# A layer of seven-product matrix multiplications: paired additions joined, marks and buffers set anew

## The chip, the cores and the metric

The kernel runs on one core of a Trainium2 chip. A core has a tensor engine (PE) for matrix products, VectorE (DVE), ScalarE (ACT) and GpSimd (POOL) for work on tiles of 128 partitions, and queues that start transfers (DMA), here mostly that of SyncE (SP). The engines work side by side, each through its own queue in order. The metric is the time of one execution on the device in microseconds (us), as the median of several runs. Shorter is better.

## The reference

The reference is one hybrid decoder layer in float32, on 256 tokens of width 2048, with 256 memory tokens:

```python
q, k, v, g_ret, xr, yr, g_a, g_b = jnp.split(rmsnorm(h) @ w_in, offsets, axis=-1)
ret_out = silu(g_ret) * head_groupnorm(chunkwise_retention(rotary(q), rotary(k), v))
rnn_out = gelu(yr) * rg_lru(causal_dwconv(xr))
merged = sigmoid(g_a) * (ret_out @ w_proj_ret) + sigmoid(g_b) * (rnn_out @ w_proj_rnn)
h = h + merged @ w_mix_out
h = h + memory_cross_attention(rmsnorm(h), rmsnorm(mem), xa_w_q, xa_w_k, xa_w_v, xa_w_o)
up = causal_dwconv(rmsnorm(h) @ w_up); gate, val = split(up)
h = h + (silu(gate) * val) @ w_down
return rmsnorm(h)
```

`w_in` has 14336 columns, `w_up` 11264, `w_down` 5632 rows, every other large weight is 2048 by 2048. Nearly all arithmetic lies in these products of 256 tokens by a weight.

## The kernel before

**Products in parts.** Each float32 operand is split into a high and a low part, and a product is three matmuls: high by high, low by high, high by low. For weights `weight_parts` does this: ACT casts a piece of `raw` to `hi` (L364), DVE subtracts it for `lo` (L365). The pool of hi and lo tiles has six of each (`PART_BUFS`), a tile holds two blocks of 128 by 512.

**Chunks and pairs.** The weights stand in one array in the order of use and come in chunks of 1 MB into three `raw` tiles, by loads on SP (L237). `weight_plan` lists the products in order. A plain one has 512 output columns. A pair has two times 512; its chunk is two blocks of 128 rows by two blocks of columns, called b11, b12, b21, b22, and it has eight chunks for 2048 rows. A chunk of a pair is worked off in `steps_pair` in one of two ways. Plain, it is 8 block products by 3 matmuls, 24 in all, of 512 columns each. Marked, it is a Strassen-like form with 7 products, 21 matmuls. A marked chunk needs on the weight's side, in `seven_parts`, four sums of blocks (L385, one DVE operation of 512 columns each) and seven parts in place of four. The token sums of its left operand are made by `sums_of` (L463 to L474), once for each left operand and kept for later products with the same one. `MARKS` lists, pair by pair in the order of the plan, which of the eight chunks are marked.

**Banks and the end of a pair.** A pair's results gather in PSUM: three tiles of two banks (pool `pm`) and two small banks (pool `px`, also used by small products). After the last marked chunk four DVE operations (L538) combine four banks into two SBUF tiles `o1`, `o2`; at the end of the pair four additions of 512 columns (L549) add the two small banks, then the two halves of the tile that holds p2 and p4.

**Order.** A step is one chunk. `chunks` loads and splits two chunks ahead (`AHEAD`) and, after each chunk, runs what `later(n, fn)` has set due n + 1 steps on. `LAG` holds these numbers for the steps around: loads of the residual rows (`rows`, `rows_step`) and of the memory rows (`squares`), the normed memory (`memory`), the head rows (`heads`), transposed rows of merged, query and key (`merge_turn`, `query_turn`, `key_turn`), the attention products (`attend`). A transposition (`by_dma`) is an ACT copy into planes, two transposing DMAs on SP and an ACT copy back. Matmuls stay in the order of the program; a planner orders the other engines' queues by priority and by when operands and buffers come free, and `high_priority` pulls the end of a pair ahead. Buffers of 4 KB a partition come from the pool `bp` ("big", 29 of them), those of 2 KB from `tp` ("tmp", 10), used by token sums, rotations, head outputs and probabilities.

**Stages.** Retention inputs and gates (until about 300 us), the recurrent branch's inputs (to 505), its projection and the gates (to 714), the retention projection and mixing (to 884), memory attention (to 1248), the feed-forward part with up and down products in turn (to 1884), and the last down product, whose four column blocks are plain.

Of the kernel before, what the change touches and what calls it, by code (L numbers as in the profile page):

```python
# [14 lines left out]
ALU = mybir.AluOpType  # L15
AX = mybir.AxisListType

P = 128
# [16 lines left out]
WARM = 7  # L35
FREE = 300
LAG = dict(
    sums=3, two_heads=2, recur=3, gelu=6, merged=2, memory=3, memory_step=3, rnn=0, rnn_step=2,
    heads=7, heads_step=1, squares=5, squares_step=1, rows=12, rows_step=1, residual=3, gate=2,
    value=4, merge_turn=2, query_turn=3, key_turn=4, turn=3, attend=1, acc_m=0, acc_h=0,  # L40
)
EPS = 1e-6
GN_EPS = 1e-5
FF_PARTS = [4, 4, 3]
EARLY = [2, 2, 4, 4, 4]
MARKS = [
    ((2, 5, 6), (3,), (3, 5, 6),),
    ((2, 5), (2, 5, 6), (2, 5, 6),),
    ((2, 4, 6), (2, 5), (2, 5), (5,),),
    ((3,), (3, 5),),  # L50
    ((), (2, 5), (2, 3), (2, 5), (2, 5), (),),
    ((5, 6), (),),
    ((2, 4), (2, 5), (5,), (2, 5), (2, 5), (2, 5), (2, 5),),
    ((2, 3, 5), (5,), (2, 5), (2, 5), (2, 5), (2, 5),),
    ((2, 5, 6), (3, 5),),
]

O_Q, O_K, O_V, O_G = 0, 1024, 2048, 4096
# [105 lines left out]
def chunk(inputs, name, row, n, c):  # L164

    if isinstance(c, tuple):
        a, b = (chunk(inputs, name, row, n, one) for one in c[:2])
        order = (b[:, 0], a[:, 0], b[:, 1], a[:, 1]) if c[2] else (a[:, 0], a[:, 1], b[:, 0], b[:, 1])
        return np.stack(order, axis=1)
    w = np.asarray(inputs[name])[0][row : row + n * P, c : c + BW].reshape(n, P, BW)  # L170
    return w.transpose(1, 0, 2)
# [9 lines left out]
def hybrid_layer(  # L181
# [18 lines left out]

    cp = ctx.enter_context(tc.tile_pool(name="cp", bufs=1))
    wp = ctx.enter_context(tc.tile_pool(name="wp", bufs=2))
    bp = ctx.enter_context(tc.tile_pool(name="bp", bufs=29))
    tp = ctx.enter_context(tc.tile_pool(name="tp", bufs=10))
    sp_ = ctx.enter_context(tc.tile_pool(name="sp", bufs=2))
    pm = ctx.enter_context(tc.tile_pool(name="pm", bufs=3, space=bass.MemoryType.PSUM))
    px = ctx.enter_context(tc.tile_pool(name="px", bufs=2, space=bass.MemoryType.PSUM))
# [13 lines left out]
    def acc():  # L221
        return pm.tile([P, 2, BW], F32, tag="acc", name=nm("acc"))
# [155 lines left out]

    def seven_parts(raw):

        b12, b11, b22, b21 = (raw[:, i, :] for i in range(4))
        p1, p3 = weight_parts(raw[:, 1:3])
        (p2,) = weight_parts(raw[:, 3:4])
        for o, a, b in ((b11, b12, b11), (b12, b12, b22), (b22, b11, b22), (b21, b22, b21)):
            dve.tensor_tensor(out=o, in0=a, in1=b, op=ALU.add)  # L385
        q3, q1 = weight_parts(raw[:, 0:2])
        q2, q4 = weight_parts(raw[:, 2:4])
        return [p1, p3, p2, q1, q3, q2, q4]

# [62 lines left out]
    def gemm_n(*args):  # L452
        return ended(steps_n(*args))
# [36 lines left out]
    def steps_pair(w, row, st, nk, c1, c2):  # L490

        seven = plan[gemms[0]][3][2]
        last = max(seven)
        banks, begun = {}, set()
        banks["p2"], banks["p4"] = (lambda a: (a[:, 0, :], a[:, 1, :]))(acc())
        banks["x3"], banks["n"] = (small((P, BW)) for _ in range(2))

        def rows_of(name, left, right, end):

            o = banks[name]  # L500
            for i, (a, b) in enumerate(((0, 0), (1, 0), (0, 1))):
                mm(o, left[a], right[b], start=name not in begun, stop=end and i == 2, skip_group_check=True)
                begun.add(name)

        o1 = o2 = None
        for k0, n, parts in chunks(nk, w, row, (c1, c2, seven)):
            k2 = k0 // KH
            for i in seven:
                if k2 < i <= k2 + LAG["sums"] and (not isinstance(st, list) or i < len(st)):
                    sums_of(st[i])  # L510
            if isinstance(st, Pairs):
                st[min(nk // KH - 1, k2 + 2)]
            t = st[k2]
            own = [
                [(t[:, j, i * P : (i + 1) * P], t[:, j, S + i * P : S + (i + 1) * P]) for j in range(2)]
                for i in range(2)
            ]
            if k2 in seven:
                if "p1" not in banks:
                    for a, b in (("p1", "p6"), ("p7", "x5")):  # L520
                        two = acc()
                        banks[a], banks[b] = two[:, 0, :], two[:, 1, :]
                ts = sums_of(t)
                s3, s1, s2, s4 = ((ts[:, 0, i, :], ts[:, 1, i, :]) for i in range(4))
                lefts = (own[0][0], s4, own[0][1], s1, s3, s2, own[1][1])
                for name, l, r in zip(("p1", "x3", "p2", "x5", "p7", "p6", "p4"), lefts, parts):
                    rows_of(name, l, r, k2 == last and name in ("p1", "x5", "p7", "p6"))
                if k2 == last:
                    o1, o2 = (big([P, 2, BW], s="o") for _ in range(2))
                    with tc.high_priority(FREE):  # L530
                        act.copy(o1[:, 0, :], banks["p1"])
                        for o, a, b, op in (
                            (o2[:, 0, :], o1[:, 0, :], banks["p6"], ALU.add),
                            (o1[:, 1, :], o2[:, 0, :], banks["p7"], ALU.add),
                            (o2[:, 1, :], banks["x5"], o1[:, 1, :], ALU.subtract),
                            (o2[:, 0, :], banks["x5"], o2[:, 0, :], ALU.subtract),
                        ):
                            dve.tensor_tensor(out=o, in0=a, in1=b, op=op)  # L538
            else:
                end = k0 + n == nk  # L540
                blocks = list(enumerate((("p2", "p4"), ("x3", "n"))))
                for b, names in reversed(blocks) if end else blocks:
                    for tt, name in enumerate(names):
                        for j in range(KH):
                            rows_of(name, own[tt][j], parts[b * KH + j], end and j == KH - 1)
            yield o1, o2
        with tc.high_priority(FREE):
            for o, a in ((o2[:, 0, :], "x3"), (o2[:, 1, :], "n"), (o1[:, 0, :], "p2"), (o1[:, 1, :], "p4")):
                dve.tensor_tensor(out=o, in0=o, in1=banks[a], op=ALU.add)  # L549

    def pair(*args):
        return ended(steps_pair(*args))
# [43 lines left out]
            for tt in range(2):  # L596
                act.mul(a[:, tt, :], a[:, tt, :], r[:, tt : tt + 1])

    def turned_rows(a, r, then, wait=1, urgent=True):

        rows = big([P, 2, BW], s="rows")
        with tc.high_priority(FREE) if urgent else nullcontext():
            for tt in range(2):
                dve.tensor_scalar_mul(rows[:, tt, :], a[:, tt, :], r[:, tt : tt + 1])  # L604
        by_dma(rows, then, wait)

    def split_pair(src, scale=None):
# [228 lines left out]
    for g in range(2):  # L836
        dec = big([P, 4, S], s="dec")
        vs, turned = [], ([], [])
        for b, o in enumerate((O_Q, O_K)):

            def rotate_both(f, o=turned[b]):
                o.append(rotated(f[:, 0:2, :]))
                later(0, lambda: o.append(rotated(f[:, 2:4, :])))

            a = gemm_n("w_in", 0, xs, NT, o + g * BW) if g + b else q0
            turned_rows(a, rs0, rotate_both, 2 - b if g + b else 3, g + b > 0)
            if b == 1:
                sp.dma_start(
                    out=dec,
                    in_=consts[:, C_DEC + g * 4 * S : C_DEC + (g + 1) * 4 * S].rearrange("p (h s) -> p h s", s=S),  # L850
                )
            if g == 0:
                v = gemm_n("w_in", 0, xs, NT, O_V + b * BW) if b else ended(v_steps)
                vs.append(split_rows(v, rs0))
        if g == 1:
            vs += [split_rows(v, rs0) for v in pair("w_in", 0, xs, NT, O_V + 1024, O_V + 1024 + BW)]
        qr, kr = turned
        gates = []
        c = O_G + g * 1024
        for a in pair("w_in", 0, xs, NT, c, c + BW):  # L860
            t = big([P, 2, BW], s="gate")
            for tt in range(2):
                act.activation(t[:, tt, :], a[:, tt, :], AF.Silu, scale=rs0[:, tt : tt + 1])
            gates.append(t)
        retain(g, qr, kr, vs, dec, gates)
# [73 lines left out]
    for b in range(4):  # L939
# [33 lines left out]
                dve.tensor_tensor(out=o, in0=xr[0][:, cs, :], in1=f[:, cs, :], op=ALU.mult)  # L973
                rnn.append(split_pair(o))

        turned_rows(gemm_n("w_in", 0, xs, NT, O_XR + b * BW), rs0, conv_x)
        turned_rows(gemm_n("w_in", 0, xs, NT, O_YR + b * BW), rs0, gelu_y, LAG["gelu"])


    def tanh_rows(t, a):  # L980
# [134 lines left out]
    def split_block(f, out, seven=()):  # L1115
        for pr in range(2):
            with_sums(out, seven, f[:, 2 * pr : 2 * pr + 2, :])
        return out
# [22 lines left out]
    def attend(b, v):  # L1141
# [4 lines left out]
        for tt in range(2):  # L1146
            cs = slice(tt * P, (tt + 1) * P)
            for kt in range(2):
                product(
                    a[:, tt, :], (phi[:, kt, cs], plo[:, kt, cs]), [t[:, kt, :] for t in v], kt == 0, kt == 1  # L1150
                )
        turned_rows(a, shares[b], lambda f: split_block(f, osp, marks_of("xa_w_o")))

    turned_pair("xa_w_k", ms, 0, rsms[0], keys)
    token_sums.clear()
# [215 lines left out]
```

## Time and profile before

| | us |
|---|---|
| median of 3 runs | 1964.05 (1963.98 to 1964.17) |
| the profiled execution | 1962.41 |
| its span | 1960.6 |
| PE busy | 1947.5 |
| weight loads busy (PEld) | 1616.5 |
| DVE busy | 1683.2 |
| ACT busy | 1426.2 |

The profile is of one execution. A group is named by line, engine, operation and the tiles it writes and reads, with shapes, count, busy time and mean duration, then the idle time of its engine just before and what ended that. An arrow in a view of waits points to the one waited for. A line is often that of a helper: all matmuls of the products are L266, all splits of weights L364 and L365. "sm" is a small bank, "acc" a tile of two banks, "ts" a token sum, "s" a split left operand. DMA moved 219 GB/s on average; the granted tensor clock was full throughout.

### The profile page before, as it was taken

How to read it: one execution, taken by the hardware profiler on the slowest of the kernel's cores; microseconds unless marked ns; L12 is line 12 of the kernel's file. 1: busy time of each engine (PE TensorE's matmuls, PEld its weight loads, DVE VectorE, ACT ScalarE, POOL GpSimd, SP SyncE). 2: the span in 40 equal slices, each digit the busy share in tenths (PEclk: the TensorE clock that was granted, in tenths of full speed). 3: DMA queues.
4: the chain of work that ended last, by engine and by line, in shares of the span. 5: the costliest groups of instructions: out<-in, count | busy, mean ns of one | idle time of the engine just before them, and what ended most of it. 6: DMA issues, size and time to landing. Idle time of an engine off the chain costs nothing.

```text
span 1960.6 us, 24200 instructions
## 1 busy us (share of the span) xinstructions
PE 1947.5 (99%) x8756; PEld 1616.5 (82%) x8756; DVE 1683.2 (86%) x2251; ACT 1426.2 (73%) x1746; POOL 35.2 (2%) x33
## 2 busy tenths in 40 slices
PE   9999999999999999999999999999999999999998
PEld 8888888888888888888888888888878888878886
DVE  6897987888799997997888668888999989998886
ACT  7666758999655766788688677887786588875783
POOL 0000011000000000000000000000000000000000
PEclk9999999999999999999999999999999999999999
DMA  9756667765555565867676656666667767677673
GB/s 337 240 215 173 205 243 205 207 226 191 199 206 195 223 240 195 308 221 243 205 220 222 211 188 202 200 231 220 204 215 229 250 217 223 207 219 253 215 238 128
DMA packets 198344, 429.82 MB, mean 219 GB/s; under 512 B 142160, under 2 KB 146768, under 8 KB 153168
## 3 DMA queue, kind: packets, MB, share of 16 engines
q1 hardware_dynamic: 197072, 424.09, 64.5%
q0 software_dynamic: 1152, 4.19, 1.2%
q8 instruction: 68, 1.11, 0.2%
q14 instruction: 52, 0.43, 0.1%
HBM read 388.39 MB, written 2.10 MB: 199 GB/s over the span
## 4 chain that ended last, share of the span: by engine, by line
PE 91%; DVE 4%; ACT 2%; issue 1%; DMA 1%; POOL 0%; POOLq 0%; DVEq 0%; SPq 0%; ACTq 0%
PE acc L266 63%; PE sm L266 28%; DVE lo L365 2%; DMA raw<-in_wall 1%; ACT hi L364 1%; DVE fv L1185 0%; DVE o L538 0%; ACT f L588 0%; DVE raw L385 0%; ACT pl L575 0%; DVE fo L1194 0%; ACT o L1311 0%; DVE o L549 0%; DMA raw<-in_head 0%; DVE fg L1185 0%
## 5 line engine op out<-in xcount | busy, mean ns | idle before, releaser
L365 DVE TENSOR_TENSOR lo<-raw,hi 128x1024 fp32r<-128x1024 f32 (+1 forms) x846 | 973.9, 1178 | 190.1 <-ACT hi L364 182.9
L364 ACT CAST hi<-raw 128x1024 fp32r<-128x1024 f32 (+1 forms) x846 | 829.4, 1012 | 368.3 <-DVE raw L385 109.6
L266 PE MATMUL acc<-hi,s 128*128 128x512 f32 (+1 forms) x3540 | 1085.1, 388 | 1.6 <-DVE s L612 1.1
L266 PEld LDWEIGHTS acc<-hi,s 128*128 128x128 f32 x3540 | 661.5, 188 | 138.1 <-DVE s L612 1.9
L266 PE MATMUL acc<-lo,s 128*128 128x512 f32 (+1 forms) x1770 | 686.2, 388 | 1.3 <-DVE lo L365 1.3
L266 PE MATMUL sm<-hi,s 128*128 128x512 f32 x1520 | 468.1, 389 | 1.1 <-DVE o L549 1.1
L266 PEld LDWEIGHTS acc<-lo,s 128*128 128x128 f32 x1770 | 332.3, 188 | 70.8 <-DVE lo L365 2.5
L266 PEld LDWEIGHTS sm<-hi,s 128*128 128x128 f32 x1520 | 285.2, 188 | 60.8 <-issue 1.5
L266 PE MATMUL sm<-lo,s 128*128 128x512 f32 x760 | 295.7, 389 | 0.0
L385 DVE TENSOR_TENSOR raw<-raw 128x512 f32<-128x512 f32 x264 | 181.4, 687 | 4.0
L588 ACT COPY f<-pt 128x1024 uint16<-128x1024 uint16 x128 | 166.4, 1353 | 9.5 <-DMA pt<-pl 9.5
L266 PEld LDWEIGHTS sm<-lo,s 128*128 128x128 f32 x760 | 142.7, 188 | 29.6
L266 PE MATMUL acc<-hi,ts 128*128 128x512 f32 x396 | 121.9, 389 | 0.0
L266 PEld LDWEIGHTS acc<-hi,ts 128*128 128x128 f32 x396 | 74.3, 188 | 15.4
L266 PE MATMUL acc<-lo,ts 128*128 128x512 f32 x198 | 77.4, 391 | 0.2 <-DVE lo L365 0.2
L575 ACT COPY pl<-o 128x1024 uint16<-128x1024 uint16 x64 | 62.6, 1040 | 2.9 <-DVE o L1043 2.2
L575 ACT COPY pl<-rows 128x1024 uint16<-128x1024 uint16 x44 | 43.8, 1042 | 17.6 <-DVE rows L604 17.5
L1311 ACT ACTIVATE o<-o,ro 128x512 f32<-128x512 f32 x44 | 30.1, 718 | 20.0 <-DVE o L549 19.5
L266 PEld LDWEIGHTS acc<-lo,ts 128*128 128x128 f32 x198 | 37.1, 188 | 9.0 <-DVE lo L365 1.5
L538 DVE TENSOR_TENSOR o<-o,acc 128x512 f32<-128x512 f32 x64 | 43.5, 680 | 0.5
L1185 DVE SCALAR_TENSOR_TENSOR fg<-f,pf,fg 128x255 f32<-128x255 f32 (+1 forms) x88 | 39.1, 478 | 4.5 <-ACT fg L1183 4.2
L549 DVE TENSOR_TENSOR o<-o,sm 128x512 f32<-128x512 f32 x64 | 42.3, 678 | 0.2
(184 smaller groups left out, 1106.5 us busy)
## 6 DMA issues: line engine op xcount, KB each, us to landing
raw<-in_wall SPq DMA_DIRECT2D x352, 1024.0 KB, 4.9
nat<-in_x SPq DMA_DIRECT2D x8, 512.0 KB, 10.2
nat<-o POOLq DMA_DIRECT2D x8, 512.0 KB, 5.7
raw<-in_wall SPq DMA_DIRECT2D x7, 512.0 KB, 5.7
pt<-pl SPq DMA_TRANSPOSE x128, 3.3
nat<-in_mem SPq DMA_DIRECT2D x4, 512.0 KB, 7.5
xt<-in_x_t SPq DMA_DIRECT2D x3, 512.0 KB, 8.9
xt<-in_mem_t SPq DMA_DIRECT2D x3, 512.0 KB, 5.6
```

Of the source, the lines that this page charges most:

```text
L266: tc.keep_in_program_order(pe.matmul(*a, **k))
L364: act.copy(hi[:, cs], src[:, cs])
L365: dve.tensor_tensor(out=lo[:, cs], in0=src[:, cs], in1=hi[:, cs].bitcast(F32), op=ALU.subtract)
L385: dve.tensor_tensor(out=o, in0=a, in1=b, op=ALU.add)
L538: dve.tensor_tensor(out=o, in0=a, in1=b, op=op)
L549: dve.tensor_tensor(out=o, in0=o, in1=banks[a], op=ALU.add)
L575: act.copy(planes[:, tt], words[:, tt])
L588: act.copy(halves_[:, :, :, cs], turned_[:, :, :, cs])
L1185: dve.scalar_tensor_tensor(out=y[:, s:S], in0=z[:, j, 0 : S - s], scalar=pf[:, 2 - s, t : t + 1], in1=y[:, s:S], op0=ALU.mult, op1=ALU.add,)
L1311: act.mul(a[:, tt, :], a[:, tt, :], rs2[:, tt : tt + 1])
```

## The change

Two pairs of DVE operations become one each. In `seven_parts` the blocks of a marked chunk are laid out in the order b11, b12, b22, b21 (the array of weights is built in that order), and the sums b12 + b11 and b12 + b22 are one operation of 1024 columns, with b12 as a repeated operand. In `steps_pair` the additions of p2 and p4 are one operation of 1024 columns on a tile of two banks. The pool `bp` gets 31 tiles for 29, `tp` 7 for 10. `MARKS` and `LAG` have other numbers. `turned_rows` gets a switch that lets ACT scale the rows; all its settings are zero.

```diff
 LAG = dict(
-    sums=3, two_heads=2, recur=3, gelu=6, merged=2, memory=3, memory_step=3, rnn=0, rnn_step=2,
-    heads=7, heads_step=1, squares=5, squares_step=1, rows=12, rows_step=1, residual=3, gate=2,
-    value=4, merge_turn=2, query_turn=3, key_turn=4, turn=3, attend=1, acc_m=0, acc_h=0,
+    sums=3, two_heads=2, recur=3, gelu=6, merged=2, memory=5, memory_step=3, rnn=0, rnn_step=2,
+    heads=6, heads_step=1, squares=6, squares_step=2, rows=13, rows_step=3, residual=3, gate=2,
+    value=4, merge_turn=1, query_turn=4, key_turn=5, turn=3, attend=3, acc_m=0, acc_h=0,
+    by_rotate=0, by_conv=0, by_gelu=0, by_attend=0,
 )
 MARKS = [
-    ((2, 5, 6), (3,), (3, 5, 6),),
-    ((2, 5), (2, 5, 6), (2, 5, 6),),
+    ((4, 5, 6), (3,), (3, 5, 6),),
+    ((2, 3, 4), (2, 5, 6), (2, 3, 5),),
     ((2, 4, 6), (2, 5), (2, 5), (5,),),
-    ((3,), (3, 5),),
-    ((), (2, 5), (2, 3), (2, 5), (2, 5), (),),
+    ((3,), (3, 6),),
+    ((), (3, 5), (2, 3), (2, 5), (4, 5), (),),
     ((5, 6), (),),
-    ((2, 4), (2, 5), (5,), (2, 5), (2, 5), (2, 5), (2, 5),),
-    ((2, 3, 5), (5,), (2, 5), (2, 5), (2, 5), (2, 5),),
-    ((2, 5, 6), (3, 5),),
+    ((2, 4), (2, 5), (3,), (2, 5), (2, 5), (2, 5), (2, 5),),
+    ((2, 3, 5), (5,), (2, 4), (2, 5), (2, 5), (2, 4),),
+    ((2, 3, 6), (2, 5),),
 ]
...
-        order = (b[:, 0], a[:, 0], b[:, 1], a[:, 1]) if c[2] else (a[:, 0], a[:, 1], b[:, 0], b[:, 1])
+        order = (a[:, 0], b[:, 0], b[:, 1], a[:, 1]) if c[2] else (a[:, 0], a[:, 1], b[:, 0], b[:, 1])
...
-    bp = ctx.enter_context(tc.tile_pool(name="bp", bufs=29))
-    tp = ctx.enter_context(tc.tile_pool(name="tp", bufs=10))
+    bp = ctx.enter_context(tc.tile_pool(name="bp", bufs=31))
+    tp = ctx.enter_context(tc.tile_pool(name="tp", bufs=7))
...
-        b12, b11, b22, b21 = (raw[:, i, :] for i in range(4))
-        p1, p3 = weight_parts(raw[:, 1:3])
+        b11, b12, b22, b21 = (raw[:, i : i + 1, :] for i in range(4))
+        p1, p3 = weight_parts(raw[:, 0:3:2])
         (p2,) = weight_parts(raw[:, 3:4])
-        for o, a, b in ((b11, b12, b11), (b12, b12, b22), (b22, b11, b22), (b21, b22, b21)):
+        two = b12.to_broadcast([P, 2, BW])
+        for o, a, b in ((raw[:, 0:2], two, raw[:, 0:3:2]), (b22, b11, b22), (b21, b22, b21)):
             dve.tensor_tensor(out=o, in0=a, in1=b, op=ALU.add)
-        q3, q1 = weight_parts(raw[:, 0:2])
+        q1, q3 = weight_parts(raw[:, 0:2])
...
-        banks["p2"], banks["p4"] = (lambda a: (a[:, 0, :], a[:, 1, :]))(acc())
+        direct = acc()
+        banks["p2"], banks["p4"] = direct[:, 0, :], direct[:, 1, :]
...
         with tc.high_priority(FREE):
-            for o, a in ((o2[:, 0, :], "x3"), (o2[:, 1, :], "n"), (o1[:, 0, :], "p2"), (o1[:, 1, :], "p4")):
-                dve.tensor_tensor(out=o, in0=o, in1=banks[a], op=ALU.add)
+            for o, a in ((o2[:, 0, :], banks["x3"]), (o2[:, 1, :], banks["n"]), (o1, direct)):
+                dve.tensor_tensor(out=o, in0=o, in1=a, op=ALU.add)
```

More of the change, by code (lines that the diff above doesn't have):

```diff
@@ L597, in scaled, with turned_rows @@
                 act.mul(a[:, tt, :], a[:, tt, :], r[:, tt : tt + 1])
-    def turned_rows(a, r, then, wait=1, urgent=True):
+    def turned_rows(a, r, then, wait=1, urgent=True, by=0):
         rows = big([P, 2, BW], s="rows")
@@ L603, in turned_rows @@
             for tt in range(2):
-                dve.tensor_scalar_mul(rows[:, tt, :], a[:, tt, :], r[:, tt : tt + 1])
+                scale = act.mul if by else dve.tensor_scalar_mul
+                scale(rows[:, tt, :], a[:, tt, :], r[:, tt : tt + 1])
         by_dma(rows, then, wait)
@@ L845, in hybrid_layer @@
             a = gemm_n("w_in", 0, xs, NT, o + g * BW) if g + b else q0
-            turned_rows(a, rs0, rotate_both, 2 - b if g + b else 3, g + b > 0)
+            turned_rows(a, rs0, rotate_both, 2 - b if g + b else 3, g + b > 0, LAG["by_rotate"])
             if b == 1:
@@ L974, in gelu_y @@
                 rnn.append(split_pair(o))
-        turned_rows(gemm_n("w_in", 0, xs, NT, O_XR + b * BW), rs0, conv_x)
-        turned_rows(gemm_n("w_in", 0, xs, NT, O_YR + b * BW), rs0, gelu_y, LAG["gelu"])
+        turned_rows(gemm_n("w_in", 0, xs, NT, O_XR + b * BW), rs0, conv_x, by=LAG["by_conv"])
+        turned_rows(gemm_n("w_in", 0, xs, NT, O_YR + b * BW), rs0, gelu_y, LAG["gelu"], by=LAG["by_gelu"])
     def tanh_rows(t, a):
@@ L1151, in attend @@
                 )
-        turned_rows(a, shares[b], lambda f: split_block(f, osp, marks_of("xa_w_o")))
+        turned_rows(a, shares[b], lambda f: split_block(f, osp, marks_of("xa_w_o")), by=LAG["by_attend"])
     turned_pair("xa_w_k", ms, 0, rsms[0], keys)
```

## The prediction

> **What bounds the kernel now.** First the page's spans and busy shares, then the waits of the tensor engine alone, then busy time by stretch, one stretch to a weight product, and last the chain that ended last and the order of time around each wait.
>
> ```profile
> span 1960.6 us, 24200 instructions
> PE 1947.5 (99%) x8756; PEld 1616.5 (82%) x8756; DVE 1683.2 (86%) x2251; ACT 1426.2 (73%) x1746; POOL 35.2 (2%) x33
> ```
> ```profile
> PE acc L266 <- DVE lo L365: 1.5, 2, 1.3
> PE acc L266 <- DVE s L612: 1.1, 2, 0.6
> PE sm L266 <- DVE o L549: 1.1, 1, 1.1
> PE warm L263 <- DVE half L1228: 1.1, 1, 1.1
> PE acc L266 <- ACT s L611: 0.3, 1, 0.3
> ```
> ```profile
> L266 PE MATMUL sm<-hi,s 128*128 128x512 f32 x1520 | 468.1, 389 | 1.1 <-DVE o L549 1.1
> ```
> ```profile
> 339.03 38.11 PE acc L266 x168
> ```
> ```profile
> 92.00:133.60 41.60, 41.60 (x186) 34.34 (x185) 41.26 (x57) 24.88 (x30) 0.00 (x0) 1.00 0.51 187
> ```
> ```profile
> 505.40:547.60 42.20, 42.20 (x188) 34.93 (x187) 34.07 (x39) 21.71 (x25) 0.00 (x0) 1.00 0.58 212
> ...
> 1417.30:1459.60 42.30, 42.30 (x187) 34.83 (x186) 40.87 (x60) 37.24 (x47) 0.00 (x0) 1.00 0.65 224
> 1459.60:1503.60 44.00, 42.68 (x187) 34.75 (x186) 41.36 (x58) 37.42 (x47) 0.00 (x0) 1.00 0.66 215
> ...
> 1714.40:1757.20 42.80, 42.61 (x187) 34.54 (x186) 39.73 (x54) 34.99 (x43) 0.00 (x0) 1.00 0.71 221
> 1757.20:1800.90 43.70, 42.56 (x187) 34.93 (x187) 39.98 (x48) 21.45 (x24) 1.73 (x2) 1.00 0.73 244
> ```
>
> The tensor engine (PE) is busy for 1947.5 of 1960.6 us. Its matmuls follow each other at a fixed pitch: 168 in 38.11 us are 0.2268 us each. In the stretches (columns: length, then PE, weight load, DVE, ACT, POOL busy, granted clock, DMA share, GB/s) PE fills its whole length nearly everywhere, at full clock. Beyond the warm-up it waited six times for 1.5 + 1.1 + 1.1 + 0.3 = 4.0 us in all. So the end is set by how many matmuls there are, plus a few waits.
>
> The second engine is VectorE (DVE). In the pair of 92 to 133.6 us it works 41.26 of 41.60 us, in the one of 1417.3 to 1459.6 us 40.87 of 42.30, in the one of 505.4 to 547.6 us only 34.07 of 42.20. Where it falls behind, PE waits:
>
> ```profile
> 1461.55 0.50 PE L266 MATMUL acc<-lo,s 128*128 128x512 f32 x1 [1.32 <-DVE lo L365]
> ```
> ```profile
> 1761.35 0.70 PE L266 MATMUL sm<-hi,s 128*128 128x512 f32 x2 [1.14 <-DVE o L549]
> ```
> ```profile
> 1918.14 0.50 PE L266 MATMUL acc<-hi,s 128*128 128x512 f32 x1 [0.56 <-DVE s L612]
> ```
>
> The first two are at the seams between two products of the feed-forward part, the third (with two like it) is where the last product waits for its left operand. A record lasts longer than the pitch (the page's mean is 0.389 us against 0.227), so each wait hides up to 0.16 us more under a neighbour: six waits are 4.0 us seen and at most 1.0 us unseen, 5.0 us in all.
>
> **The change part by part.**
>
> *Marks.* I counted the marked chunks in the two lists: 66 before (264 sum operations, four to a chunk, below), 67 after; the first rnn projection has three in place of two, other pairs change places only. A marked chunk has 21 matmuls for 24. One more takes 3 x 0.2268 = **0.68 us** off PE, and this lies on the path, since PE has no slack there.
>
> ```profile
> L365 DVE TENSOR_TENSOR lo<-raw,hi 128x1024 fp32r<-128x1024 f32 x774 | 927.9, 1224 | 187.3 <-ACT hi L364 180.1 <-PE sm L266 2.2
> L385 DVE TENSOR_TENSOR raw<-raw 128x512 f32<-128x512 f32 x264 | 181.4, 687 | 4.0
> ```
> ```profile
> 507.42 2.87 DVE L385 TENSOR_TENSOR raw<-raw 128x512 f32<-128x512 f32 x4
> ```
> ```profile
> 1440.84 0.69 DVE L385 TENSOR_TENSOR raw<-raw 128x512 f32<-128x512 f32 x1
> 1441.44 0.48 DVE L1185 SCALAR_TENSOR_TENSOR fg<-f,pf,fg 128x255 f32<-128x255 f32 x1
> ```
> ```profile
> 325.33 2.36 DVE L365 TENSOR_TENSOR lo<-raw,hi 128x1024 fp32r<-128x1024 f32 x2 [1.90 <-ACT hi L364]
> ```
>
> *The two joined weight sums.* A sum of 512 columns holds the queue for 0.60 us where other work stands behind it (1440.84 to 1441.44), and for (2.87 - 0.69) / 3 = 0.73 us where the next sum needs its result. Two subtractions of 1024 take 2.36 us, so one holds it for 2.36 - 1.22 = 1.14 us. The joined sum has no row of its own; its form, fp32 and 1024 columns with two inputs, is nearest to that subtraction, and I take its 1.14 us. A marked chunk saves 2 x 0.60 - 1.14 = 0.06 us where the scheduler had put other work between the sums, and up to 2 x 0.73 - 1.14 = 0.32 us where all four ran back to back (if the joined one pays no wait for its own result; with one like the sums now, 0.13 us, it is 0.19). The repeated operand could also cost something: if the second half ran as a second operation, the saving is zero. Over 66 chunks that is 0 to 21 us of DVE time, and I take 0.06 to 0.19, 4 to 13 us. The form of the reads for ACT changes too (every second block of the chunk), with the same element count; I take no cost.
>
> ```profile
> 1761.73 1.27 DVE L549 TENSOR_TENSOR o<-o,acc 128x512 f32<-128x512 f32 x2
> ```
>
> *The two joined final additions.* Two of 512 take 1.27 us, the joined one 1.22 by the subtraction above; in queue time 2 x 0.60 - 1.14 = 0.06 us, for 32 pairs 2 us. The two additions that free the small banks still come first, so PE's wait on L549 at 1761.35 gains nothing from it.
>
> ```profile
> L463 DVE TENSOR_TENSOR g<-s 128x512 f32<-128x512 f32 x25 | 17.1, 683 | 0.4 <-PE sm L266 0.4
> ```
> ```profile
> L474 DVE TENSOR_TENSOR ts<-tq,ts x31: 674/683/694, 103.0 to 1807.5; 128x512 fp32r<-128x512 f32 x31
> L469 DVE TENSOR_TENSOR tq<-g x25: 409/417/426, 98.8 to 1799.6; 128x256 f32<-128x256 f32 x25
> L470 DVE TENSOR_TENSOR tq<-tq,g x25: 263/282/293, 99.7 to 1801.7; 128x128 f32<-128x128 f32 x25
> L471 DVE TENSOR_TENSOR tq<-g,tq x25: 278/283/293, 101.7 to 1804.9; 128x128 f32<-128x128 f32 x25
> ```
>
> *What the new marks cost DVE.* A left operand that is used in some marked chunk gets its token sums once. By the lists there are 31 before (the x31 of L474) and 34 after: one more each for the rnn rows, the memory rows and the second part of the hidden rows. One is 0.68 + 0.42 + 0.28 + 0.28 + 0.68 = 2.3 us of durations, so 3 are 7 us. The 67th marked chunk costs 3 x 1.14 + 0.60 + 2.5 of sums less the 2 x 1.14 of a plain one, about 4 us. So DVE gets back 6 to 15 us and spends 11: its total stays where it was within 5 us of 1683. The relief is local, about 0.1 to 0.4 us for a pair with two marks.
>
> *The waits.* In front of the wait at 1461.55 DVE is full of such work (40.87 us of the stretch's 42.30) and the marks of that pair stay; relief of 0.1 to 0.4 us shortens a wait of 1.32 by that much. That is the low end. But the order of DVE's queue is planned over the whole kernel, and the two seam waits exist only because a subtraction or an addition came behind some half a dozen others. With moved marks they may close altogether: 1.32 + 1.14 + 0.19 (the rest of the waits on L365) plus 0.16 unseen for each of three is 3.1 us. Between nothing and 3.1 I take the half, **1.5 us**, since nothing says which. Three waits at the end (1.4 us) stay: there the left operand is late by the chain behind the last up-projection, which changes only in two marks.
>
> ```profile
> SPq L237 <- DVE lo L365: 1282.8, 306, 12.2
> ...
> SPq L237 <- DVE tq L471: 34.1, 5, 10.7
> ```
> ```profile
> raw<-in_wall SPq DMA_DIRECT2D x352, 1024.0 KB, 4.9
> nat<-in_x SPq DMA_DIRECT2D x8, 512.0 KB, 10.2
> ...
> pt<-pl SPq DMA_TRANSPOSE x128, 3.3
> nat<-in_mem SPq DMA_DIRECT2D x4, 512.0 KB, 7.5
> ```
>
> *Two more big tiles, three fewer small ones, and the moved steps.* Loads on the sync queue (SP) waited 34.1 us for a big tile to come free after token sums, in front of weight loads; with two more tiles some of that goes. No PE wait stands behind it, so the gain is 0. The small tiles drop from 10 to 7. The most I count live at once is seven (four head outputs with the probabilities and a token sum), so 7 is just enough and I take 0; one stage held up for a tile would cost PE what a seam wait does, 1.3 us. The steps that get another due time are the transposes of merged, query and key rows (on SP, 3.3 us each), the loads of the residual and memory rows (10.2 and 7.5 us on SP), the normed memory, the head rows, the squares and the attention products. All fall where PE waits for nothing, between 505 and 1250 us, and every weight load queued behind a moved DMA has cover: 306 times the loads stood waiting for a raw buffer, up to 12.2 us, and not for the queue. I take 0 for them. If a load of 10.2 us came when the raw buffers are empty, the loss is that less the two chunks worked ahead, about 0. The new `by` switches are all zero and change nothing.
>
> **Sum.** -0.68 - 1.5 = -2.2 us. The profiled execution took 1962.41 us (its span and 1.8 around it), 1.64 less than the median of the runs; the difference is carried over: 1964.05 - 2.2 = **1961.8 us**. That is 0.11% faster, inside the 0.2% (3.9 us) that a measurement of this kernel tells from no change.
>
> **The rivals.**
>
> A, all waits close: the six go with what they hide, 5.0 us, and 0.68: 1958.4 us. For it: they are thin. Against: the three at the end are a chain of transposes and convolutions that the change hardly touches.
>
> B, DVE sets the pace, and PE merely looks full. Then DVE's net change comes through whole: 15 - 11 = 4 us, or, with the 0.32 us of the back-to-back bound, 21 + 2 - 11 = 12 us, so 1952 to 1960. Against it: the 168 matmuls in one run at 0.2268 us. [...]
>
> C, slower: three marked chunks in a row. The gate pair of 92 to 133.6 us goes from chunks 2, 5, 6 to 4, 5, 6 and the rnn projection at 505.4 from 2, 5 to 2, 3, 4. A marked chunk asks DVE for 3 x 1.14 + 0.60 + 2.5 = 6.5 us and PE for 21 x 0.2268 = 4.76, so each falls 1.7 us behind, three 5.2. The six part buffers hold one and a half marked chunks, 7.1 us of PE. It decides when more than 7.1 - 5.2 = 1.9 us of other DVE work falls into those 14 us: two token sums are 4.6 us, 2.7 too much. For one or two such places, with the same again where DVE catches up late in the next pair, I estimate 5.4 us: 1964.05 - 0.68 + 5.4 = 1968.8. For it: DVE at 41.26 of 41.60 in the first. Against: two in a row pass now without a PE wait, and the plain chunks ahead (24 x 0.2268 = 5.44 us of PE, 2 x 1.14 of DVE) give DVE 3.1 us each to get ahead with the sums.
>
> D, the change does nothing but drop three matmuls, or shifts a wait elsewhere: 1963.4 to 1964.1.
>
> **How the numbers follow.** My forecast 0.40 (own range 1960.3, with all three seam waits gone, to 1963.4, with none), A 0.22, B 0.05, C 0.20, D 0.13. Faster is A and B, 0.27; within 0.2% the forecast and D, 0.53; slower C, 0.20. The range leaves out the lower part of A and B (some 0.1) and the upper half of C (0.1): 1957.8 to 1968.8.
>
> **What would show it.** PE with about three matmuls fewer, 67 joined sums near 1.22 us, 34 token sums, DVE's busy time within some 1% of before. The seam waits near 1460 and 1760 us shorter or gone, those near 1918 us still there. Wrong would be: new PE waits in the stretches around 120 or 520 us, a joined sum well over 1.3 us, or PE waits named after tiles freed late.

## The result

| | before | after |
|---|---|---|
| median of ten runs, us | 1964.37 (1963.84 to 1967.15) | 1959.64 (1959.18 to 1960.31) |
| the profiled execution, us | 1962.41 | 1959.31 |
| its span, us | 1960.6 | 1957.5 |

The ratio after to before is 0.9974, with a 95% interval of 0.9964 to 0.9984: 4.7 us by the medians, faster by 0.26%. The two profiled executions differ by only 3.1 us, because the one of before was quicker than all ten of its timed runs. What follows reads the profiles for places and the medians for sizes.

First the page of the changed kernel, then the waits of its tensor engine:

```profile
span 1957.5 us, 24123 instructions
...
PE 1946.6 (99%) x8753; PEld 1617.4 (83%) x8753; DVE 1684.9 (86%) x2173; ACT 1432.0 (73%) x1751; POOL 35.1 (2%) x33
```
```profile
PE warm L264 <- DVE half L1232: 1.1, 1, 1.1
PE acc L267 <- DVE lo L366: 0.8, 1, 0.8
PE acc L267 <- DVE s L616: 0.2, 1, 0.2
```

There are three matmuls fewer (8753 for 8756), VectorE is as busy as before (1684.9 us for 1683.2), and of the six waits with 4.0 us, two with 1.0 us are left. The remaining seam wait has its old place and cause:

```profile
1461.17 0.50 PE L267 MATMUL acc<-lo,s 128*128 128x512 f32 x1 [0.82 <-DVE lo L366]
```

In the stretches (columns as in the prediction) PE fills its time where three marked chunks stand in a row, and at the old seam near 1760 us:

```profile
92.00:133.60 41.60, 41.60 (x185) 34.48 (x184) 41.13 (x55) 24.84 (x29) 0.00 (x0) 1.00 0.50 184
505.40:547.60 42.20, 42.20 (x188) 34.95 (x187) 40.93 (x50) 24.90 (x29) 0.00 (x0) 1.00 0.57 208
...
1459.60:1503.00 43.40, 42.58 (x188) 34.94 (x187) 40.12 (x52) 36.32 (x45) 0.00 (x0) 1.00 0.68 218
...
1757.20:1800.90 43.70, 43.70 (x194) 36.22 (x193) 42.55 (x51) 21.29 (x25) 2.60 (x3) 1.00 0.78 262
```

The joined operations, by lines and forms:

```profile
L387 DVE TENSOR_TENSOR raw<-raw 128x512 f32<-128x512 f32 x134 | 92.4, 689 | 2.2
L387 DVE TENSOR_TENSOR raw<-raw 128x1024 f32<-128x1024 f32 x67 | 81.9, 1223 | 0.6
...
L552 DVE TENSOR_TENSOR o<-o,acc 128x1024 f32<-128x1024 f32 x32 | 39.0, 1220 | 0.7 <-PE acc L267 0.6
```
```profile
524.02 2.67 DVE L387 TENSOR_TENSOR raw<-raw 128x1024 f32<-128x1024 f32 x3
```

67 joined sums take 1.223 us each, the joined final additions, which repeat no operand, 1.220: the repeated operand costs nothing here. Where the sums of a chunk run back to back they take 2.67 us in place of 2.87. The profiled spans balance like this: 0.7 us of matmuls and about 4.2 us of waits are gone (3.0 of them in the lists of waits; the rest, counted from the starts of the matmuls, is hidden under neighbouring records or too short for the lists). About 0.8 us is lost in the first ten matmuls after the warm-up, which came at a slower pitch in this execution, and about 0.9 us after the last matmul, which starts at 1948.48 of 1957.5 us (before: 1952.52 of 1960.6). That leaves 3.1.

```profile
4.51 2.15 PE L267 MATMUL acc<-hi,s 128*128 128x512 f32 x4
```
```profile
4.50 1.47 PE L266 MATMUL acc<-hi,s 128*128 128x512 f32 x4
```

The first row is after, the second before: the same four matmuls, 0.7 us apart. It belongs to the execution and not to the kernel: in the repeat of the changed kernel, below, they took 1.46 us.

### The profile page after: what moved, and what is told of

The parts are those of the page before. It is cut to its first block, busy times and chain, and to the rows that moved or that the text cites. A ratio compares the mean times of both kernels' runs of the same rounds, so it can differ in the third digit from the quotient of the medians.

```text
span 1957.5 us, 24123 instructions
## 1 busy us (share of the span) xinstructions
PE 1946.6 (99%) x8753; PEld 1617.4 (83%) x8753; DVE 1684.9 (86%) x2173; ACT 1432.0 (73%) x1751; POOL 35.1 (2%) x33
## 4 chain that ended last, share of the span: by engine, by line
PE 90%; DVE 5%; ACT 2%; issue 2%; DMA 1%; POOLq 0%; POOL 0%; DVEq 0%; SPq 0%; ACTq 0%
PE acc L267 63%; PE sm L267 27%; DVE lo L366 2%; DMA raw<-in_wall 1%; ACT hi L365 1%; DVE fv L1189 1%; DVE o L541 0%; DVE o L552 0%; ACT f L591 0%; DVE fg L1189 0%; DVE raw L387 0%; DVE fo L1198 0%; DVE s L616 0%; ACT pl L578 0%; DMA raw<-in_head 0%
## 5 line engine op out<-in xcount | busy, mean ns | idle before, releaser
L387 DVE TENSOR_TENSOR raw<-raw 128x512 f32<-128x512 f32 (+1 forms) x201 | 174.3, 867 | 2.7
```

## The experiments

Two theories at first. **M**: the count of matmuls and a few waits make the time, and the new marks and due times close the waits. **J**: the joins relieve VectorE, and that closes them. The kernel before ran beside each batch, with medians of 1964.74, 1965.10 and 1964.69 us; ratios are to it.

| kernel | median, us | ratio to before, 95% |
|---|---|---|
| joins alone | 1966.01 | 1.0009 (1.0000 to 1.0018) |
| changed, no joins | 1959.37 | 0.9970 (0.9959 to 0.9981) |
| changed, old marks | 1965.57 | 1.0004 (0.9995 to 1.0013) |
| changed, old numbers of tiles | 1962.82 | 0.9990 (0.9981 to 0.9999) |
| changed, old due times | 1957.27 | 0.9965 (0.9951 to 0.9978) |
| changed, weight sums left out | 1955.22 | 0.9954 (0.9940 to 0.9967) |
| before, new marks alone | 1962.16 | 0.9987 (0.9979 to 0.9996) |
| before, new numbers of tiles alone | 1964.59 | 1.0000 (0.9992 to 1.0009) |
| changed, ten marks removed | 1972.46 | 1.0040 (1.0027 to 1.0053) |
| before, new marks and tiles | 1957.75 | 0.9963 (0.9951 to 0.9976) |
| changed, old due times, three marks more | 1966.44 | 1.0005 (0.9996 to 1.0014) |
| changed, once more | 1959.35 | 0.9970 (0.9959 to 0.9980) |

### Do the joins carry the gain?

The kernel before with both joins, and nothing else:

```diff
...
-        for o, a, b in ((b11, b12, b11), (b12, b12, b22), (b22, b11, b22), (b21, b22, b21)):
+        two = b12.to_broadcast([P, 2, BW])
+        for o, a, b in ((raw[:, 0:2], two, raw[:, 0:3:2]), (b22, b11, b22), (b21, b22, b21)):
...
-            for o, a in ((o2[:, 0, :], "x3"), (o2[:, 1, :], "n"), (o1[:, 0, :], "p2"), (o1[:, 1, :], "p4")):
+            for o, a in ((o2[:, 0, :], banks["x3"]), (o2[:, 1, :], banks["n"]), (o1, direct)):
```

> The kernel before with the two joins alone; marks, due times and buffers as before. Theory M (the time is the count of matmuls plus a few waits, and it is the new marks and due times that close the waits): no matmul less, the waits near 1460 and 1760 us shorter by 0.1 to 0.4 us each, so 0.2 to 0.8 us under the kernel before. Theory J (the joins relieve VectorE, and that closes the waits): most of the 4.4 to 4.7 us, so 3.5 to 4.5 us under it.

Measured: 1.3 us above the kernel before, at the edge of what tells from no change. No gain: theory J falls, and so does the part of M that gave the joins 0.2 to 0.8 us. The profile shows a wait that the kernel before did not have, in its list of tensor engine waits and near 104 us in the order of time:

```profile
PE sm L266 <- DVE ts L475: 1.2, 1, 1.2
```
```profile
96.50 1.22 DVE L386 TENSOR_TENSOR raw<-raw 128x1024 f32<-128x1024 f32 x1
...
100.66 0.68 DVE L464 TENSOR_TENSOR g<-s 128x512 f32<-128x512 f32 x1
...
105.12 0.69 DVE L475 TENSOR_TENSOR ts<-tq,ts 128x512 fp32r<-128x512 f32 x1
```

VectorE's order in the kernel before, at the same place:

```profile
96.33 0.68 DVE L385 TENSOR_TENSOR raw<-raw 128x512 f32<-128x512 f32 x1
96.92 0.68 DVE L463 TENSOR_TENSOR g<-s 128x512 f32<-128x512 f32 x1
...
103.00 0.68 DVE L474 TENSOR_TENSOR ts<-tq,ts 128x512 fp32r<-128x512 f32 x1
```

Before, the planner put the steps of the token sum (L463 to L474) between the four short sums, and its last step began at 103.00. With the joined sum the first step comes at 100.66 in place of 96.92, the last at 105.12 in place of 103.00, and the first matmul that needs what the last step writes waits 1.2 us. The changed kernel with the marks of before has the same wait; with chunks 4, 5 and 6 marked the wait is gone, with the joins and without them.

The other side, the changed kernel with both joins undone:

```diff
...
-        for o, a, b in ((raw[:, 0:2], two, raw[:, 0:3:2]), (b22, b11, b22), (b21, b22, b21)):
+        for o, a, b in ((b11, b12, b11), (b12, b12, b22), (b22, b11, b22), (b21, b22, b21)):
...
-            for o, a in ((o2[:, 0, :], banks["x3"]), (o2[:, 1, :], banks["n"]), (o1, direct)):
+            for o, a in ((o2[:, 0, :], "x3"), (o2[:, 1, :], "n"), (o1[:, 0, :], "p2"), (o1[:, 1, :], "p4")):
```

> The changed kernel with both joins undone; marks, due times and buffers stay new. Theory M: 3.5 to 4.5 us under the kernel before. Theory J: with 67 marked chunks and three more token sums on an unrelieved VectorE no gain is left, 0 to 4 us above the kernel before.

1959.37 us, what the changed kernel takes. With new marks the joins are worth nothing either.

### Marks

> The changed kernel with the marks of before; joins, due times and buffers stay new. Three matmuls more, 0.68 us. Theory M: the seam waits come back, 2 to 4 us above the changed kernel. Theory J: 0.7 us above it, no more.

```diff
-    ((4, 5, 6), (3,), (3, 5, 6),),
-    ((2, 3, 4), (2, 5, 6), (2, 3, 5),),
+    ((2, 5, 6), (3,), (3, 5, 6),),
+    ((2, 5), (2, 5, 6), (2, 5, 6),),
...
```

1965.57 us: the whole gain is gone, 5.9 us by the medians, of which 0.7 are matmuls. The marks' part of theory M holds, and by more than it expected; its part on the due times does not, as shown below. The new marks alone on the kernel before:

> The kernel before with the new marks alone; no joins, old due times, old buffers. If the marks alone close the waits: 3.5 to 5 us under the kernel before. Theory S (marks need the two big tiles): 0.5 to 2.5 us under it. If marks were chosen for the other settings and are bad without them: at the kernel before or above it.

2.9 us under it, a little over the range for "marks need the two big tiles".

### Numbers of tiles

> The changed kernel with 29 big and 10 small tiles as before. Theory M and J as the prediction has it: the buffers are worth nothing, within 0.5 us of the changed kernel. Rival K (the two big tiles close the waits, since loads behind a missing big tile come late): 1.5 to 4 us above the changed kernel.

```diff
-    bp = ctx.enter_context(tc.tile_pool(name="bp", bufs=31))
-    tp = ctx.enter_context(tc.tile_pool(name="tp", bufs=7))
+    bp = ctx.enter_context(tc.tile_pool(name="bp", bufs=29))
+    tp = ctx.enter_context(tc.tile_pool(name="tp", bufs=10))
```

3.2 us above the changed kernel: I had them at nothing, and here rival K was right. But alone they do nothing:

> The kernel before with 31 big and 7 small tiles alone. Rival K (a missing big tile delays what the seams wait for): 1.5 to 3 us under the kernel before. Theory S (the tiles only help the new marks): within 1 us of it. If seven small tiles are too few with the old marks: above it, with PE waits that end with a token sum or a head output.

1964.59 us, no change: theory S, not K. Together with the new marks, and without joins and new due times, they give the gain:

> The kernel before with the new marks and the new numbers of tiles; no joins, old due times. If the gain of the kernel with old due times is that of marks and tiles: 1957 to 1958.5 us. If the joins give a part there that they do not give under the new due times: 1959 to 1961.5 us, between the marks alone (1962.16) and the kernel with joins and old due times (1957.27).

1957.75 us. That is 4.4 us under the marks alone and as quick as any kernel with joins. The two differ in nothing but the two pool sizes. What happens at the seam near 1505 us, first with marks alone (its two longest waits of the tensor engine, then VectorE in order of time):

```profile
PE sm L266 <- DVE o L549: 1.6, 1, 1.6
...
PE acc L266 <- DVE o L538: 1.0, 1, 1.0
```
```profile
1488.63 1.66 DVE L1185 SCALAR_TENSOR_TENSOR fg<-f,pf,fg 128x255 f32<-128x255 f32 x4
...
1503.40 0.68 DVE L538 TENSOR_TENSOR o<-o,acc 128x512 f32<-128x512 f32 x1
...
1508.07 1.27 DVE L549 TENSOR_TENSOR o<-o,sm 128x512 f32<-128x512 f32 x2
```

And with marks and tiles:

```profile
1480.94 2.45 DVE L1185 SCALAR_TENSOR_TENSOR fg<-f,pf,fg 128x255 f32<-128x255 f32 x6
...
1497.84 0.68 DVE L538 TENSOR_TENSOR o<-o,acc 128x512 f32<-128x512 f32 x1
...
1504.07 1.28 DVE L549 TENSOR_TENSOR o<-o,sm 128x512 f32<-128x512 f32 x2
```

With the other pool sizes six of the gate convolution's operations run at 1480.94, and the operations that free the banks come 5.6 and 4.0 us sooner; both waits are gone. Why the convolution starts earlier shows one step back, where ACT copies the finished pair into planes for the transposing DMAs (L575). First with marks alone, then with marks and tiles:

```profile
1464.37 1.98 ACT L575 COPY pl<-o 128x1024 uint16<-128x1024 uint16 x2
...
1473.67 1.99 ACT L575 COPY pl<-o 128x1024 uint16<-128x1024 uint16 x2 [1.10 <-DMA pt<-pl]
```
```profile
1465.41 3.87 ACT L575 COPY pl<-o 128x1024 uint16<-128x1024 uint16 x4
```

With marks alone the second half of the copies comes 9.3 us after the first and waits for a DMA that reads a planes tile. The copies read only `o`, which was complete at 1464.5 us, and write only planes, which are big tiles; so the wait is for a big tile to come free, and the rows for the convolution are turned late. The changed kernel with the old numbers of tiles shows the same gap (copies at 1466.61 and 1476.74 us, the second after a wait of 1.22 us) and the same two waits of 1.6 and 1.0 us behind it. At this seam it is thus the big tiles. The two pools were not changed one at a time, so what the three fewer small tiles do by themselves stays open. Nor is this seam the whole account: marks and tiles have a wait of 1.4 us near 1461 us that marks alone do not have, and their profiled executions differ by 2.6 us, where the medians differ by 4.4.

### Due times

> The changed kernel with the due times of before; joins, marks and buffers stay new. Theory S (the gain sits in the marks and the two big tiles together; due times matter only through the order they cause): 0 to 2 us above the changed kernel. Rival L (the due times carry a part of their own, as the undone buffers did with some 3 us): 2.5 to 5 us above it.

```diff
-    sums=3, two_heads=2, recur=3, gelu=6, merged=2, memory=5, memory_step=3, rnn=0, rnn_step=2,
-    heads=6, heads_step=1, squares=6, squares_step=2, rows=13, rows_step=3, residual=3, gate=2,
-    value=4, merge_turn=1, query_turn=4, key_turn=5, turn=3, attend=3, acc_m=0, acc_h=0,
+    sums=3, two_heads=2, recur=3, gelu=6, merged=2, memory=3, memory_step=3, rnn=0, rnn_step=2,
+    heads=7, heads_step=1, squares=5, squares_step=1, rows=12, rows_step=1, residual=3, gate=2,
+    value=4, merge_turn=2, query_turn=3, key_turn=4, turn=3, attend=1, acc_m=0, acc_h=0,
```

1957.27 us, 2.4 under the changed kernel by the medians; all five runs (1956.27 to 1958.05) lie below its first ten, though its later eight begin at 1957.36. The two ran in different batches and the intervals of their ratios overlap, so this says that the new due times bring nothing, and more likely cost a little. With the old ones the profile has one wait of PE left, 0.5 us. Of the kernels that leave nothing out this one and the one with marks and tiles alone are the quickest.

### Is it the count of matmuls or VectorE?

> The changed kernel without the three operations of weight sums in each of the 67 marked chunks: the four combined blocks are left as they are, so their products are of the wrong weights, with the same count of matmuls. VectorE is freed of about 170 us. Theory M (the count of matmuls sets the time): only the remaining waits of some 3 us can go, so 1 to 4 us under the changed kernel. Rival B of the prediction (VectorE sets the pace): 20 us or more under it.

```diff
-        two = b12.to_broadcast([P, 2, BW])
-        for o, a, b in ((raw[:, 0:2], two, raw[:, 0:3:2]), (b22, b11, b22), (b21, b22, b21)):
-            dve.tensor_tensor(out=o, in0=a, in1=b, op=ALU.add)
```

```profile
span 1953.5 us, 23911 instructions
...
PE 1944.8 (100%) x8753; PEld 1617.7 (83%) x8753; DVE 1532.7 (78%) x1972; ACT 1433.2 (73%) x1751; POOL 34.0 (2%) x33
```

VectorE works 152 us less, and 4.4 us of the time go (M said 1 to 4), with the last wait of the tensor engine outside its warm-up. Rival B is out. 1955.2 us is what this list of matmuls takes without waits; the changed kernel is 0.2% above it. The reverse, ten marks taken away:

> The changed kernel with ten marked chunks made plain again in the seven pairs from the first rnn projection to the last retention projection, where the tensor engine waits for nothing and VectorE is busy 34 to 42 of 42 us. Theory M (the count of matmuls sets the time): 30 matmuls of 0.2268 us more, 6.8 us above the changed kernel, although VectorE is freed of some 45 us or more. Rival B (VectorE sets the pace): below the changed kernel.

```diff
-    ((2, 3, 4), (2, 5, 6), (2, 3, 5),),
-    ((2, 4, 6), (2, 5), (2, 5), (5,),),
+    ((2,), (2,), (2,),),
+    ((2,), (2,), (2,), (5,),),
```

13.1 us above the changed kernel of the same batch, with VectorE 48 us less busy (1636.4 us): above it, as M says, but twice the 6.8 of the matmuls. Most of the rest is a wait that the edit made. Only the first of the two retention projections decides which head rows get their token sum early; its list now lacks 5, so the second projection made that sum itself, too late:

```profile
796.16 1.52 PE L267 MATMUL sm<-hi,ts 128*128 128x512 f32 x2 [5.69 <-ACT ts L475]
```
```profile
796.10:799.20 3.10, 3.04 (x7) 2.12 (x8) 1.10 (x2) 1.20 (x3) 0.00 (x0) 0.50 0.75 312
799.20:805.00 5.80, 5.80 (x27) 4.82 (x26) 5.29 (x6) 3.63 (x5) 0.00 (x0) 0.98 0.47 155
```

So the price of a mark by itself was not measured cleanly; 6.8, 5.7 and some 1.5 for the matmuls after it, at a granted clock of 0.50 in the first row, are 14.0 together, near the 13.1.

### More marks

> The changed kernel with old due times and three more marked chunks, in pairs where VectorE is idle for 6.6 to 7.1 us (the second retention projection, the second key pair, the seventh up pair). Theory M: nine matmuls less, 2.0 us under the kernel with old due times, so 1955.2 us, if 4 us of VectorE work a chunk fit into the idle time. If the new order of the queue makes a wait: 1956 to 1959 us.

```diff
-    ((2, 4, 6), (2, 5), (2, 5), (5,),),
+    ((2, 4, 6), (2, 5), (2, 5), (2, 5),),
...
-    ((), (3, 5), (2, 3), (2, 5), (4, 5), (),),
+    ((), (3, 5), (2, 3), (2, 4, 5), (4, 5), (),),
...
-    ((2, 3, 5), (5,), (2, 4), (2, 5), (2, 5), (2, 4),),
+    ((2, 3, 5), (2, 5), (2, 4), (2, 5), (2, 5), (2, 4),),
```

9.2 us above the kernel it was made from by the medians (some 8 by the ratios, as the two ran in different batches), and outside both ranges, although 9 matmuls are gone and VectorE had been idle 6.6 to 7.1 us in each of the three pairs. The waits, before them the page's busy times:

```profile
PE 1948.4 (99%) x8744; PEld 1614.3 (82%) x8744; DVE 1696.2 (86%) x2188; ACT 1433.3 (73%) x1757; POOL 36.0 (2%) x33
```
```profile
PE acc L267 <- DVE lo L366: 3.9, 5, 1.2
PE sm L267 <- DVE o L552: 1.1, 1, 1.1
...
PE acc L267 <- DVE s L619: 0.8, 1, 0.8
```

The waits add up to 7.1 us beyond the warm-up, against 0.5 in the kernel it was made from; counted from the starts of the matmuls, delays too short for the list included, some 11 us more are lost, which cover the 2.0 saved and the rest. Idle time summed over a pair was no room. Only three of the waits, near 788, 1052 and 1061 us, lie in pairs that got a mark (1.1, 1.2 and 0.5 us); the others lie where the marks were not touched, one of 1.1 us near 676 us, ahead of all three pairs. So it is the new order of the queue that costs; why that order came out so much worse stays open.

### The changed kernel again

> The changed kernel once more, as the measure for the three others on their chip: 1959.6 us within 0.7, and the waits of the profiled execution at the same places, near 1460 and 1916 us.

1959.35 us, with the waits near 1460 and 1916 us. The places are those of the first profile; they belong to the order of the queues, not to chance.

## Why the prediction was right or wrong

**The range and the bound were right.** 1959.64 lies in 1957.8 to 1968.8, and what PE is given to do sets the time, shown by the run without weight sums (1955.22 us with VectorE 152 us less busy). The call was less good: forecast were 2.2 us and "within 0.2%" (0.53); 4.7 us came, 0.26%, so that 1959.64 lies just below the forecast's own range (1960.3 to 1963.4), between it and rival A (1958.4), to which I had given 0.22.

**Marks, -0.68 us:** as counted, 8753 for 8756.

**Cost of VectorE's parts:** right. The joined sum was put at a row of 1024 columns and measured 1.223 us; back to back it saves 0.20 (0.19 taken). The joins took 10.4 us off VectorE's busy time (1696.0 us with marks, tiles and no joins, 1685.6 with joins and old due times, the rows below), in the 6 to 15 forecast, and the three token sums and the added mark spent it: 1684.9 for 1683.2.

```profile
PE 1946.4 (99%) x8753; PEld 1616.9 (83%) x8753; DVE 1696.0 (87%) x2272; ACT 1430.6 (73%) x1751; POOL 36.0 (2%) x33
```
```profile
PE 1945.2 (100%) x8753; PEld 1616.7 (83%) x8753; DVE 1685.6 (86%) x2173; ACT 1429.8 (73%) x1751; POOL 34.5 (2%) x33
```

**The waits, -1.5 us: the step that was mis-sized.** About 4.2 us went in the profiled executions. The prediction looked for this to the moved marks; the runs give it to the marks and the numbers of tiles together. "Between nothing and 3.1 I take the half" was about right for the seams: the one near 1760 closed, the one near 1460 fell from 1.32 to 0.82. "Three waits at the end (1.4 us) stay" was wrong: one of 0.2 us is left. I took the chain behind the last up-projection to be independent of the marks; the same marks with other due times or tiles left between nothing and 0.6 us there, so it depends on the order of the queues and not on the marks alone.

**"No PE wait stands behind it, so the gain is 0" (two more big tiles): wrong.** The pool sizes are worth 3.2 us in the changed kernel and 4.4 with marks alone, and nothing with the old marks. My argument looked at which PE waits of before ended with a missing tile. The tiles act on waits that the new marks would otherwise have brought, and not in front of PE: near 1465 us an ACT copy waits for a big tile, the turned rows come late, and VectorE's operations that free the banks come late with them.

**Due times, 0:** within what can be told, with signs of a small cost.

**Rival C did not happen.** Three marked chunks in a row run without a PE wait at VectorE 41.13 of 41.60 us. A price of its kind was seen elsewhere: three more marks made the kernel 9.2 us slower, although they save 2.0.

**The joins** I gave a local relief that shortens waits. The 10.4 us freed on VectorE brought none (1966.01 us with the joins alone, 1964.74 before), and the coarser grain made a wait of 1.2 us at one place with the old marks.

## What to carry to other kernels

With the tensor engine busy 99% of the span, 10 us saved on a second engine at 86% were worth nothing by themselves; what counted was the order of its queue near the few waits, and a join of two operations can take away the place between them where a planner had put urgent work (here a wait of 1.2 us). Buffer counts and placement act together: here the tiles gave 0 alone, the marks 2.9, both 7 us, so test such settings in pairs before calling one idle. Idle time summed over a stage does not show that more work fits: three marks put where VectorE was idle for 6.6 to 7.1 us cost 9.2 us.

## What the runs showed of the hardware

After the wait of 5.69 us in the run with ten marks removed the granted tensor clock was 0.50 for the 3.1 us of the first row shown there, in which seven matmuls were counted, and 0.98 on average over the 5.8 us after it. In the kernel before it was 1.00 for the 3.1 us behind the wait of 1.32 us near 1461 us, with fourteen matmuls. The long wait so cost about 1.5 us more than itself, an estimate from 3.1 us at a clock of 0.50. The next longest wait of the tensor engine in the lists of all runs is 1.8 us (the changed kernel with old marks), so how long a wait must be for such a drop is not shown. The first four matmuls after the warm-up took 2.15 us in one execution and 1.47 and 1.46 us in two others; that this is the clock too is not shown, as the clock's column says 1.00 there (4.5 to 8.0 us of the changed kernel).

A two-input operation whose first operand is one block read twice, and whose output overlaps that operand, ran at the rate of an ordinary one (1.223 us for 1024 columns, 1.226 for the subtraction).

```profile
L366 DVE TENSOR_TENSOR lo<-raw,hi 128x1024 fp32r<-128x1024 f32 x775 | 931.4, 1226 | 174.2 <-ACT hi L365 166.8 <-PE acc L267 2.7
```
